# Stores moved to ScalarE's queue, a three-buffer decay pipeline and a gate row summed on GpSimd in a hybrid encoder layer

## The chip, the cores and the metric

The kernel runs on one core of one Trainium2 chip, in one launch. A core has five engines that run their own instruction streams side by side and meet through semaphores: TensorE (PE), VectorE (DVE), ScalarE (ACT), GpSimd (POOL) and SyncE (SP). SP only issues DMA transfers; ACT and POOL can issue them too, each on a queue of its own, in the order of its stream. The metric is the device time of the whole program in microseconds (us), as a median of several runs; less is better.

## What is computed

One layer of a bidirectional hybrid encoder in float32, for 2048 tokens of width 1024. The reference, cut to what the change touches:

```python
mod = c_act @ w_ada[l] + b_ada[l]
shift, scale, gate = jnp.split(mod, 3, axis=-1)
h = rmsnorm(h_res, norm_w[l]) * (1.0 + scale[:, None, :]) + shift[:, None, :]
proj = h @ w_in + b_in
(na_q, na_k, na_v, na_z, ml_q, ml_k, ml_v, ml_o, ml_z, i_f, f_f, i_b, f_b) = jnp.split(proj, split_idx, axis=-1)
na_out = neighbourhood_attention(na_q, na_k, na_v, rpb) * jax.nn.silu(na_z)
qk = jax.nn.silu(centred_short_conv(jnp.concatenate([ml_q, ml_k], axis=-1), conv_w, conv_b))
...
lower = jnp.tril(jnp.ones((L, L), dtype=bool))
Dlog = jnp.where(lower, b[..., :, None] - b[..., None, :] + i_pre[..., None, :], -jnp.inf)
...
S = jnp.einsum('bhntd,bhnsd->bhnts', q, k) * jnp.exp(Dlog - m_t[..., None])
...
hm = (h_fwd + h_bwd).transpose(0, 2, 1, 3) * jax.nn.sigmoid(ml_o).reshape(B, T, ML_HEADS, ML_HEAD_DIM)
...
y = jnp.concatenate([na_out, ml_out], axis=-1) @ w_out
...
h_res = h_res + gate[:, None, :] * y
return rmsnorm(h_res, final_norm_w)
```

`gate` is a row of 1024 numbers, the last third of an adaptive modulation (adaLN); the kernel multiplies it into `w_out` once instead of into every output row. The `exp(Dlog - m_t)` factors, one 64x64 triangle for each chunk, head and direction, are the "decays".

## The kernel before

Every large projection is done in three matmul passes for float32 accuracy: weights and activations are split into a high part (`whi`, `hhi`) and a low part (`wlo`, `hlo`), and hi·hi, lo·hi and hi·lo are added in PSUM (lines 429 to 431). A block of 256 weight columns is loaded in two halves of 512 KB by `load_w` (L193, on SP), ACT makes the high part (L195) and POOL the low part (L196). There are two slots for split weights: `whi_a`/`wlo_a` for even blocks and `whi_b`/`wlo_b` for odd ones, so that the weights of a block are fetched while the block before is computed.

The stages around the change, in PE's order:

- **Start.** Blocks 0 and 1 (mLSTM value and output gate of heads 0 and 1, with the gate columns) run while the rows of x arrive, are normalised (sum of squares on ACT into `junk`, L223) and transposed into `hhi`/`hlo` (L287 to L292). `table_fills` (L538) writes a constant into the bias tables `d_t` in HBM, on SP's queue.
- **Value stage** (`tok_blocks`). Blocks 2 and 3 (`vo_group`: value and output gate of heads 2 and 3) and blocks 4 and 5 (`nav_group`: value of the neighbourhood attention), token-major: 16 tiles of 24 matmuls with 256 columns each. DVE evacuates each tile with a bias (L499, L464) into a staging tile of four (`stvo`, `stv`; two buffers), the output gate gets its sigmoid on ACT (L503), and the staging tile is stored from SP's queue (L506, L468). The store of a group is put off by `defer` and issued by `flush` one group later. After every tile, `next(self.chain)` runs one step of side work: first `gate_chain` (the log-gate arithmetic), then `decays`: for each of 16 groups two broadcast loads (L702, SP), the triangle mask on POOL (L710), eight exponentials (L714) and two stores on ACT's queue (L716), with two buffers. In the steps in between, `gate_row` loads `w_ada`'s gate columns 128 rows at a time into the two halves of `wide` (L401, SP) and sums them on DVE (L408, L410), adds them over partitions with a matmul against a column of ones (L418) and writes the finished row to HBM (`d_gate`); it also copies the final norm weight to `d_fnw`.
- **Convolution** (`conv_blocks`). Blocks 6 and 7 (k) and 8 and 9 (q), channel-major: 8 tiles a block, each 24 matmuls with 512 columns. ACT evacuates a tile with its bias into `u` (L773), DVE passes the two border columns to and from the neighbouring tile (L777, L778) and runs the five taps into `acc` (L806, L808), ACT applies Silu (L809), SP stores the result (L813). For k, PE then transposes it (L819), ACT scales it into `stk` (L821) and SP stores that (L823). A tile's taps need its right neighbour's first columns, so they run a tile later. `conv_step` advances all tiles that are under way by one step. Side work here is `gated_out`: it loads `w_out` in 16 half rows (L737), DVE multiplies the gate in (L744), SP stores the product in `d_wo` (L745). Table rows (`tables_rows`, L551, 72 small copies within HBM, on SP) are spread over blocks 6 to 8.
- **Phase 1b.** The first further projection `pq` (L865) starts right after the last convolution tile. Its weights come by `nq_load` (L830, `rawq`, 512 KB for each 128 columns) and are split by ACT (L838) and POOL (L839) into slot a. The first load is called at the start of block 9, whose own weights are in slot b. The mLSTM scan follows, whose loads `kv` (L1016) and `ck` (L1061) read what the stages before have stored in `d_ck`.

All dependences are found by the tile framework from the tiles' names and buffers; it also orders the instructions of each engine by a model of its own, so that a queue's order in the built program isn't always that of the code. Every DMA of SP and ACT signals one of eight semaphores, taken in turn, and its instruction first waits until the DMA that had that semaphore before has completed.

Of the kernel before, what the change touches and what calls it, by code (L numbers as in the profile page):

```python
# [8 lines left out]
F32 = mybir.dt.float32  # L9
# [6 lines left out]
P = 128  # L16
# [46 lines left out]
class Kernel:  # L63
# [30 lines left out]
    def scratch(self):  # L94
# [10 lines left out]
        self.d_fnw = d.tile([1, D], F32, name="d_fnw")  # L105
        self.d_gate = d.tile([1, D], F32, name="d_gate")
# [284 lines left out]
    def gate_row(self, pool):  # L391

        nc = self.nc
        cact = pool.tile([P, KT], F32, name="cact2")
        nc.sync.dma_start(cact, self.cT)
        nc.scalar.activation(cact, cact, AF.Silu)
        acc = pool.tile([P, D], F32, name="gsum")
        buf = [self.wide[:, :D], self.wide[:, D:]]

        def load(kt):  # L400
            nc.sync.dma_start(buf[kt % 2], self.w_ada[kt * P : (kt + 1) * P, 2 * D : 3 * D])  # L401

        load(0)
        load(1)
        yield
        for kt in range(KT):
            if kt == 0:
                nc.vector.tensor_scalar(acc, buf[0], cact[:, kt : kt + 1], None, ALU.mult)  # L408
            else:
                nc.vector.scalar_tensor_tensor(acc, buf[kt % 2], cact[:, kt : kt + 1], acc, ALU.mult, ALU.add)  # L410
            if kt + 2 < KT:
                load(kt + 2)
            yield
        row = buf[0][0:1]
        nc.sync.dma_start(row, self.b_gate)
        for j in range(2):
            ps = self.sp.tile([P, GT], F32, tag="sp", name=f"gp_{j}")
            nc.tensor.matmul(ps[0:1, :], self.ones[:, 0:1], acc[:, j * GT : (j + 1) * GT], start=True, stop=True)  # L418
            yield
            nc.vector.tensor_add(row[:, j * GT : (j + 1) * GT], row[:, j * GT : (j + 1) * GT], ps[0:1, :])  # L420
        nc.sync.dma_start(self.d_gate, row)
        row = buf[1][0:1]
        nc.sync.dma_start(row, self.fnw)
        nc.sync.dma_start(self.d_fnw, row)

# [31 lines left out]
    def nav_group(self, blk, slot, g):  # L457
# [10 lines left out]
        self.defer(lambda: nc.sync.dma_start(dst, st[:, :, :256]))  # L468
# [16 lines left out]
    def vo_group(self, h, slot, g, first=None):  # L485
        nc = self.nc
        st = self.stage_tile(f"stvo_{h}_{g}")
        nc.gpsimd.memset(st[:, :, 128:129], 1.0)
# [88 lines left out]
    def gate_chain(self, pool, gates):  # L577
# [101 lines left out]
        for i, (name, src) in enumerate((("g", g), ("w", w_r), ("inter", in_r), ("guard", gu_r))):  # L679
            t = self.gtile[:, 1 + i].rearrange("p (d h c) -> p d h c", d=2, h=MH)  # L680
            nc.vector.tensor_copy(t.rearrange("p d h c -> p (d h c)"), transposed(src, f"c_{name}"))
            self.cols[name] = t
            yield

    def decays(self, pool, beside):

        nc = self.nc
        mask = pool.tile([P, 2, CH], F32, name="mask")
# [965 lines left out]
```

## Time and profile before

| | us |
|---|---|
| median of 3 runs | 1388.04 |
| lowest, highest | 1387.38, 1388.36 |
| the profiled execution | 1394.31 |
| its span (first to last instruction) | 1392.3 |
| start: blocks 0, 1 | 0 to 160 |
| value stage: blocks 2 to 5 | 160 to 357 |
| convolution: blocks 6 to 9 | 357 to 554 |
| phase 1b and all that follows | 554 to 1392 |

Times in the profile count from the start of the span. A row of a timeline or of the groups names the line of the code, the engine, the operation, output <- inputs, shapes and the count; in brackets stands how long the engine had been idle before it and what released it. "SPq" and "ACTq" rows are DMA instructions in a queue's issuing engine: their duration is the time the instruction held the queue, not the transfer. The wait table says who waited for whom: total, times, longest.

### The profile page before, as it was taken

Reading aid. Unit: us, or ns where it says so; the run is one execution under the profiler, and the core shown is the slowest. Engines: PE = TensorE matmul, PEld = TensorE weight load, DVE = VectorE, ACT = ScalarE, POOL = GpSimd, SP = SyncE. Lnnn points to the kernel's source line nnn. Section 1 sums busy time; section 2 is a strip of 40 time slices with the busy share of each in tenths; the row PEclk is TensorE's granted clock in tenths of the full one; section 3 lists DMA queues with packets and bytes.
Section 4 is the critical chain, followed back from the end, with each engine's and each line's share of the span. In section 5 each row is a group of like instructions: output and inputs, shape, how many; then the busy total and the mean of one; then the engine's idle time right before and its main releaser. Section 6 shows DMA issues by size and latency. Waiting matters only on the chain.

```text
span 1392.3 us, 23366 instructions
## 1 busy us (share of the span) xinstructions
PE 1307.3 (94%) x8076; PEld 1124.4 (81%) x8076; DVE 823.7 (59%) x2497; ACT 528.7 (38%) x1131; POOL 293.7 (21%) x323
## 2 busy tenths in 40 slices
PE   2989999997999899999999999799998999999996
PEld 2989998987877787888878787688876888888885
DVE  6683323211255559156867777877636776777673
ACT  4642334523233323112323313233335555555551
POOL 4453222424101010001212002112402211111121
PEclk9999999999999999999999999999999999999999
DMA  9799439778458685565766888846687896876872
GB/s 317 224 288 226 121 108 230 187 193 192 135 111 216 145 186 159 170 168 146 201 191 204 247 233 226 211 131 185 177 242 232 188 226 162 198 196 169 190 182 61
DMA packets 269723, 263.68 MB, mean 189 GB/s; under 512 B 33482, under 2 KB 230090, under 8 KB 269606
## 3 DMA queue, kind: packets, MB, share of 16 engines
q1 hardware_dynamic: 178062, 186.45, 50.3%
q0 software_dynamic: 21520, 37.73, 11.0%
q10 hardware_dynamic: 70024, 38.02, 9.7%
q8 instruction: 64, 1.05, 0.3%
q14 instruction: 53, 0.43, 0.1%
HBM read 177.57 MB, written 92.72 MB: 194 GB/s over the span
## 4 chain that ended last, share of the span: by engine, by line
PE 51%; DMA 6%; DVE 4%; issue 3%; ACT 1%; POOL 1%; SPq 0%; ACTq 0%; POOLq 0%; DVEq 0%
PE pq L865 17%; PE y L1435 13%; PE pO L1396 4%; PE pT L1381 4%; DMA kv<-d_ck 3%; PE pc L430 2%; PE pc L431 2%; PE pc L429 2%; PE pS L1353 2%; PE px L1091 2%; PE pi L1093 2%; PE pS L1354 2%; PE dc L1039 1%; DMA d_qna<-qst 1%; PE a L1078 1%
## 5 line engine op out<-in xcount | busy, mean ns | idle before, releaser
L865 PE MATMUL pq<-hhi,whi_a 128*128 128x512 f32 x512 | 208.3, 407 | 2.1 <-ACT whi_a L841 1.3
L865 PE MATMUL pq<-hhi,wlo_a 128*128 128x512 f32 x512 | 208.2, 407 | 0.5 <-DVE wlo_a L842 0.5
L865 PE MATMUL pq<-hlo,whi_a 128*128 128x512 f32 x512 | 208.6, 407 | 0.0
L1360 ACT ACTIVATE pbuf<-pbuf,mn 128x480 f32<-128x480 f32 (+5 forms) x128 | 76.3, 597 | 103.3 <-DVE mn L1359 103.1
L865 PEld LDWEIGHTS pq<-hhi,whi_a 128*128 128x128 f32 x512 | 97.4, 190 | 20.1 <-ACT whi_a L841 1.8
L865 PEld LDWEIGHTS pq<-hhi,wlo_a 128*128 128x128 f32 x512 | 97.3, 190 | 17.8 <-DVE wlo_a L842 1.0
L865 PEld LDWEIGHTS pq<-hlo,whi_a 128*128 128x128 f32 x512 | 97.1, 190 | 16.5
L1435 PE MATMUL y<-hhi,whi_a 128*128 128x512 f32 x256 | 86.1, 405 | 3.1 <-ACT hhi L1334 2.8
L1435 PE MATMUL y<-hhi,wlo_a 128*128 128x512 f32 (+1 forms) x272 | 85.1, 386 | 0.2 <-ACT y L1442 0.2
L1359 DVE CUSTOM_DVE_ANT_0 pbuf<-pS,tab 128x480 f32<-128x480 f32 (+5 forms) x128 | 65.1, 541 | 32.6 <-PE pS L1354 24.2
L839 POOL TENSOR_TENSOR wlo_a<-rawq,whi_a 128x1024 fp32r<-128x1024 f32 x20 | 48.1, 2406 | 165.9 <-ACT whi_a L838 124.2
L1115 POOL TENSOR_TENSOR hm<-hm,ck 128x128 f32<-128x128 f32 x64 | 26.3, 412 | 264.1 <-DVE hm L1114 188.8
L429 PE MATMUL pvo<-whi_b,hhi 128*128 128x256 f32 x256 | 74.8, 292 | 5.3 <-DVE stvo L499 5.3
L1096 ACT ACTIVATE num<-px,gtile 128x129 f32<-128x129 f32 x120 | 38.2, 365 | 99.5 <-PE px L1091 83.5
L1023 DVE TENSOR_SCALAR wv<-kv,gtile 128x129 f32<-128x129 f32 x120 | 39.1, 333 | 60.9 <-DMA kv<-d_ck 31.9
L430 PE MATMUL pvo<-wlo_b,hhi 128*128 128x256 f32 x256 | 73.6, 287 | 0.0
L431 PE MATMUL pvo<-whi_b,hlo 128*128 128x256 f32 x256 | 73.5, 287 | 0.0
L714 ACT ACTIVATE dec<-dec,gtile 128x128 f32<-128x128 f32 x128 | 42.1, 392 | 72.3 <-POOL dec L710 63.4
L499 DVE TENSOR_TENSOR stvo<-pvo,brow 128x256 f32<-128x256 f32 x64 | 26.5, 420 | 70.0 <-PE pvo L431 56.2
L464 DVE TENSOR_TENSOR stv<-pv,brow 128x256 f32<-128x256 f32 x32 | 12.4, 421 | 90.2 <-DMA d_vna<-stv 49.1
L1396 PE MATMUL pO<-pt,v 128*64 128x128 f32 (+3 forms) x832 | 60.8, 282 | 0.0
L1381 PE MATMUL pT<-ident,pbuf 128*128 128x128 f32 (+2 forms) x416 | 59.1, 280 | 0.0
(302 smaller groups left out, 3573.0 us busy)
## 6 DMA issues: line engine op xcount, KB each, us to landing
ck<-d_ck SPq DMA_DIRECT2D x64, 384.5 KB
kv<-d_ck SPq DMA_DIRECT2D x120, 128.5 KB
rawq<-in_w_main_dram SPq DMA_DIRECT2D x28, 512.0 KB
raw<-in_w_main_dram SPq DMA_DIRECT2D x20, 512.0 KB
d_ck<-stvo SPq DMA_DIRECT2D x16, 514.0 KB
x<-in_x_dram SPq DMA_DIRECT2D x16, 512.0 KB
wada<-in_w_ada_dram SPq DMA_DIRECT2D x32, 256.0 KB
dec<-d_mneg SPq DMA_DIRECT2D x32, 256.0 KB
```

Of the source, the lines that this page charges most:

```text
L429: nc.tensor.matmul(ps, lhi(k), rhi(k), start=(k == 0), stop=False)
L430: nc.tensor.matmul(ps, lhi(k), rlo(k), start=False, stop=False)
L431: nc.tensor.matmul(ps, llo(k), rhi(k), start=False, stop=(k == KT - 1))
L714: nc.scalar.activation(t[:, d, o, :], t[:, d, o, :], AF.Exp, bias=self.cols["g"][:, d, h, c : c + 1])
L839: nc.gpsimd.tensor_tensor(lo[:, :, cs], raw, hi[:, :, cs].bitcast(F32), ALU.subtract)
L865: nc.tensor.matmul(patch_ps(ps) if patch else ps, w, self.htok(h, g, k, patch), start=(k == 0 and n == 0), stop=(k == KT - 1 and n == 2))
L1023: nc.vector.tensor_scalar(wv, tiles[d, i][:, 128:257], self.cols["w"][:, d, h, c : c + 1], None, ALU.mult)
L1359: nc.vector.tensor_tensor_reduce(pt[:, :nk], ps, tabs[place[u]][j][:, :nk], 1.0, 3e38, ALU.add, ALU.min, mn)
L1360: nc.scalar.activation(pt[:, :nk], pt[:, :nk], AF.Exp, bias=mn, scale=-1.0, accum_out=sums[:, j : j + 1])
L1381: nc.tensor.transpose(ps[:cs, i, :], pts[j][:, i * cs : (i + 1) * cs], self.ident)
L1396: nc.tensor.matmul(po[j * HD : (j + 1) * HD, :], v[:n, h * HD : (h + 1) * HD], pt[j][:n, i, :], start=(i == 0), stop=(i == nch - 1))
L1435: nc.tensor.matmul(y, m[:, k, :], w[k][:, cs], start=(k == 4 and n == 0), stop=(k == 3 and n == 2))
```

## The change

The gate row leaves the value stage: `gate_row`, `d_gate` and `d_fnw` are gone, and the final norm weight is read from the input when it is used. `gated_out` now begins by loading 16 half rows (128x512) of `w_ada`, and POOL scales and sums them; one matmul against a full matrix of ones for each half sums over partitions and broadcasts, and DVE adds the bias. `w_out`'s halves come after that, so `gated_out` has 32 items instead of 16 and its later ones fall later in the stage.

The decays use a third buffer (the `gsum` tile's tag) and are laid out as a pipeline: a group's load, its mask three steps later and its exponentials and stores five steps later, with a new group every two and a half steps.

The stores `d_vna`, `d_ck<-stvo`, `d_ck<-acc` and `d_ck<-stk` are issued from ACT's queue; those of `stvo` and `acc` right behind the instruction on ACT that makes the tile. The one-column memset of `stvo` goes from POOL to DVE. In the convolution one more step of `gated_out` is taken before each tile, and the k transpose comes one step later.

```diff
--- before.py
+++ after.py
@@ -102,8 +102,6 @@
         self.d_kna = d.tile([2, 512, T], F32, name="d_kna")
         self.d_mix = d.tile([16, P, 4, P], F32, name="d_mix")
         self.d_wo = d.tile([KT, P, D], F32, name="d_wo")
-        self.d_fnw = d.tile([1, D], F32, name="d_fnw")
-        self.d_gate = d.tile([1, D], F32, name="d_gate")
@@ -388,41 +386,6 @@
             pass
         self.flush()
 
-    def gate_row(self, pool):
-
-        nc = self.nc
-        cact = pool.tile([P, KT], F32, name="cact2")
-        nc.sync.dma_start(cact, self.cT)
-        nc.scalar.activation(cact, cact, AF.Silu)
-        acc = pool.tile([P, D], F32, name="gsum")
-        buf = [self.wide[:, :D], self.wide[:, D:]]
-
-        def load(kt):
-            nc.sync.dma_start(buf[kt % 2], self.w_ada[kt * P : (kt + 1) * P, 2 * D : 3 * D])
-
-        load(0)
-        load(1)
-        yield
-        for kt in range(KT):
-            if kt == 0:
-                nc.vector.tensor_scalar(acc, buf[0], cact[:, kt : kt + 1], None, ALU.mult)
-            else:
-                nc.vector.scalar_tensor_tensor(acc, buf[kt % 2], cact[:, kt : kt + 1], acc, ALU.mult, ALU.add)
-            if kt + 2 < KT:
-                load(kt + 2)
-            yield
-        row = buf[0][0:1]
-        nc.sync.dma_start(row, self.b_gate)
-        for j in range(2):
-            ps = self.sp.tile([P, GT], F32, tag="sp", name=f"gp_{j}")
-            nc.tensor.matmul(ps[0:1, :], self.ones[:, 0:1], acc[:, j * GT : (j + 1) * GT], start=True, stop=True)
-            yield
-            nc.vector.tensor_add(row[:, j * GT : (j + 1) * GT], row[:, j * GT : (j + 1) * GT], ps[0:1, :])
-        nc.sync.dma_start(self.d_gate, row)
-        row = buf[1][0:1]
-        nc.sync.dma_start(row, self.fnw)
-        nc.sync.dma_start(self.d_fnw, row)
-
     def mm3(self, ps, lhi, llo, rhi, rlo):
         nc = self.nc
         for k in range(KT):
@@ -465,7 +428,7 @@
             next(self.chain, None)
         self.flush()
         dst = self.d_vna[g * GT : (g + 1) * GT, c0 : c0 + 256].rearrange("(o p) c -> p o c", p=P)
-        self.defer(lambda: nc.sync.dma_start(dst, st[:, :, :256]))
+        self.defer(lambda: nc.scalar.dma_start(dst, st[:, :, :256]))
 
     def load_bias(self, blk):
         self.nc.sync.dma_start(self.brows[blk % 2], self.b_row[0:1, 256 * blk : 256 * blk + 256].broadcast_to([P, 256]))
@@ -485,7 +448,7 @@
     def vo_group(self, h, slot, g, first=None):
         nc = self.nc
         st = self.stage_tile(f"stvo_{h}_{g}")
-        nc.gpsimd.memset(st[:, :, 128:129], 1.0)
+        nc.vector.memset(st[:, :, 128:129], 1.0)
         brow = self.brows[h % 2]
         width = 272 if h == 0 else 256
         for o in range(4):
@@ -502,8 +465,7 @@
             next(self.chain, None)
         nc.scalar.activation(st[:, :, 129:257], st[:, :, 129:257], AF.Sigmoid)
         self.flush()
-        dst = self.d_ck[h, 4 * g : 4 * g + 4, :, 128:385].rearrange("o p c -> p o c")
-        self.defer(lambda: nc.sync.dma_start(dst, st[:, :, 0:257]))
+        nc.scalar.dma_start(self.d_ck[h, 4 * g : 4 * g + 4, :, 128:385].rearrange("o p c -> p o c"), st[:, :, 0:257])
 
 
     def tables_begin(self, pool):
@@ -556,7 +518,7 @@
 
     def tok_blocks(self, chain_pool):
         self.wide = chain_pool.tile([P, 2 * D], F32, name="wide")
-        self.chain = itertools.chain(self.gate_chain(chain_pool, self.gates), self.decays(chain_pool, self.gate_row(chain_pool)))
+        self.chain = itertools.chain(self.gate_chain(chain_pool, self.gates), self.decays(chain_pool))
         order = [2, 3, 4, 5]
         self.tables_begin(chain_pool)
         for n, blk in enumerate(order):
@@ -682,7 +644,7 @@
             self.cols[name] = t
             yield
 
-    def decays(self, pool, beside):
+    def decays(self, pool):
 
         nc = self.nc
         mask = pool.tile([P, 2, CH], F32, name="mask")
@@ -694,7 +656,7 @@
 
         def load(n):
             h, gi = groups[n]
-            flat = pool.tile([P, D], F32, tag=("wgate", "gacc")[n % 2], bufs=1, name=f"dec_{h}_{gi}")
+            flat = pool.tile([P, D], F32, tag=("wgate", "gacc", "gsum")[n % 3], bufs=1, name=f"dec_{h}_{gi}")
             t = flat.rearrange("p (d c t) -> p d c t", d=2, c=4)
             for d in range(2):
                 r = d * 64 + h * NC + 4 * gi
@@ -702,51 +664,69 @@
                 nc.sync.dma_start(flat[:, d * 512 : (d + 1) * 512], src.broadcast_to([P, 512]))
             tiles[n] = t
 
-        load(0)
-        load(1)
-        yield
-        for n, (h, gi) in enumerate(groups):
+        def masked(n):
+            nc.gpsimd.tensor_tensor(tiles[n], tiles[n], mask.unsqueeze(2).broadcast_to([P, 2, 4, CH]), ALU.add)
+
+        def exponent(n):
+            h, gi = groups[n]
             t = tiles.pop(n)
-            nc.gpsimd.tensor_tensor(t, t, mask.unsqueeze(2).broadcast_to([P, 2, 4, CH]), ALU.add)
             for d in range(2):
                 for o in range(4):
                     c = 4 * gi + o
                     nc.scalar.activation(t[:, d, o, :], t[:, d, o, :], AF.Exp, bias=self.cols["g"][:, d, h, c : c + 1])
                 dst = self.d_ck[h, 4 * gi : 4 * gi + 4, :, 641 + d * CH : 641 + (d + 1) * CH].rearrange("c p t -> p c t")
                 nc.scalar.dma_start(dst, t[:, d])
+
+        ends = [5 * n // 2 for n in range(len(groups))]
+        for step in range(ends[-1] + 6):
+            for fn, late in ((exponent, 5), (masked, 3), (load, 0)):
+                if step - late in ends:
+                    fn(ends.index(step - late))
             yield
-            next(beside, None)
-            yield
-            if n + 2 < len(groups):
-                load(n + 2)
-            yield
-        for _ in beside:
-            pass
 
     def gated_out(self, pool):
 
         nc = self.nc
+        cact = pool.tile([P, KT], F32, name="cact2")
+        nc.sync.dma_start(cact, self.cT)
+        nc.scalar.activation(cact, cact, AF.Silu)
         gate = pool.tile([P, D], F32, name="gate")
-        nc.sync.dma_start(gate, self.d_gate.broadcast_to([P, D]))
-        halves = [(k, slice(j * GT, (j + 1) * GT)) for k in range(KT) for j in range(2)]
+        nc.sync.dma_start(gate, self.b_gate.broadcast_to([P, D]))
+        columns = [slice(j * GT, (j + 1) * GT) for j in range(2)]
+        sums = [(kt, j, self.w_ada[kt * P : (kt + 1) * P, 2 * D + j * GT : 2 * D + (j + 1) * GT]) for j in range(2) for kt in range(KT)]
+        halves = [(k, j, self.w_out[:, k, cs]) for k in range(KT) for j, cs in enumerate(columns)]
+        todo = sums + halves
         raws = {}
 
         def load(n):
-            k, cs = halves[n]
-            raws[n] = pool.tile([P, GT], F32, tag="wraw", bufs=2, name=f"wraw_{n}")
-            nc.sync.dma_start(raws[n], self.w_out[:, k, cs])
+            if n < len(todo):
+                raws[n] = pool.tile([P, GT], F32, tag="wraw", bufs=2, name=f"wraw_{n}")
+                nc.sync.dma_start(raws[n], todo[n][2])
 
         load(0)
         load(1)
         yield
-        for n, (k, cs) in enumerate(halves):
+        for n, (k, j, _) in enumerate(todo):
             raw = raws.pop(n)
-            nc.vector.tensor_tensor(raw, raw, gate[:, cs], ALU.mult)
-            nc.sync.dma_start(self.d_wo[k][:, cs], raw)
+            cs = columns[j]
+            if n >= len(sums):
+                nc.vector.tensor_tensor(raw, raw, gate[:, cs], ALU.mult)
+                nc.sync.dma_start(self.d_wo[k][:, cs], raw)
+            elif k == 0:
+                acc = pool.tile([P, GT], F32, tag="gsum", bufs=1, name=f"gsum_{j}")
+                nc.gpsimd.tensor_scalar(acc, raw, cact[:, k : k + 1], None, ALU.mult)
+            else:
+                nc.gpsimd.tensor_scalar(raw, raw, cact[:, k : k + 1], None, ALU.mult)
+                nc.gpsimd.tensor_tensor(acc, acc, raw, ALU.add)
+                if k == KT - 1:
+                    ps = self.sp.tile([P, GT], F32, tag="sp", name=f"gp_{j}")
+                    nc.tensor.matmul(ps, self.ones, acc, start=True, stop=True)
+                    yield
+                    nc.vector.tensor_add(gate[:, cs], gate[:, cs], ps)
             yield
-            if n + 2 < len(halves):
-                load(n + 2)
-            yield
+            load(n + 2)
+            if n >= len(sums):
+                yield
 
 
     def conv_blocks(self, pool):
@@ -767,6 +747,7 @@
                 ct = 2 * pair + sub
                 bias = self.bcol[:, (12 if kind == "q" else 16) + ct : (13 if kind == "q" else 17) + ct]
                 for g in range(NG):
+                    next(self.chain, None)
                     ps = self.pp.tile([P, GT], F32, tag="pp", name=f"pc_{blk}_{sub}_{g}")
                     self.ch_tile(ps, self.wslot[slot], sub, g)
                     last, u = u if g else None, pool.tile([P, GT + 4], F32, tag="u", bufs=4, name=f"u_{blk}_{sub}_{g}")
@@ -807,10 +788,10 @@
             else:
                 nc.vector.scalar_tensor_tensor(acc, src, w, acc, ALU.mult, ALU.add)
         nc.scalar.activation(acc, acc, AF.Silu, bias=self.cb[:, cc : cc + 1])
-        yield
         j = 0 if kind == "q" else 1
         dst = self.d_ck[ct, 4 * g : 4 * g + 4, :, 385 + j * CH : 385 + (j + 1) * CH].rearrange("c p t -> p c t")
-        nc.sync.dma_start(dst, acc.rearrange("p (c t) -> p c t", t=CH))
+        nc.scalar.dma_start(dst, acc.rearrange("p (c t) -> p c t", t=CH))
+        yield
         yield
         if kind == "q":
             return
@@ -820,7 +801,7 @@
         st = self.stage_tile(f"stk_{ct}_{g}")[:, :, 0:128]
         nc.scalar.activation(st, ps.rearrange("p (a q) -> p a q", a=4), AF.Copy, scale=KSCALE)
         d2 = self.d_ck[ct, 4 * g : 4 * g + 4, :, 0:128].rearrange("o p c -> p o c")
-        nc.sync.dma_start(d2, st)
+        nc.scalar.dma_start(d2, st)
 
 
     def nq_load(self, i, s):
@@ -1286,7 +1267,7 @@
 
         def load_fnw():
             fnw.append(self.qst.tile([P, 1032], F32R, tag="st", name="fnw")[:, :D])
-            nc.sync.dma_start(fnw[0].bitcast(F32), self.d_fnw.broadcast_to([P, D]))
+            nc.sync.dma_start(fnw[0].bitcast(F32), self.fnw.broadcast_to([P, D]))
 
         def load_z(b):
             nc.gpsimd.dma_start(zs[pos[b] % 2], self.d_zna[b])
```

## The prediction

> **What bounds the kernel now.** I read the page's engine table first, then a table of stretches cut at the stages (value projections to 357, convolution to 554, then phase 1b), then the waits of 190 to 560, then timelines at the waits found.
>
> ```profile
> PE 1307.3 (94%) x8076; PEld 1124.4 (81%) x8076; DVE 823.7 (59%) x2497; ACT 528.7 (38%) x1131; POOL 293.7 (21%) x323
> ...
> 228.00:250.00 22.00, 17.05 (x127) 16.42 (x125) 8.56 (x9) 9.21 (x23) 4.94 (x4) 0.92 0.78 218
> 250.00:357.00 107.00, 98.17 (x791) 95.56 (x792) 14.95 (x38) 40.77 (x104) 35.70 (x15) 0.97 0.79 193
> 357.00:480.00 123.00, 120.66 (x565) 97.77 (x564) 60.95 (x123) 34.81 (x52) 9.65 (x4) 1.00 0.58 140
> 480.00:500.00 20.00, 17.52 (x73) 13.86 (x72) 13.88 (x22) 7.18 (x10) 5.78 (x2) 0.91 0.70 199
> 500.00:556.00 56.00, 55.22 (x238) 44.50 (x237) 48.17 (x91) 16.55 (x25) 5.00 (x2) 1.00 0.72 176
> ```
>
> TensorE (PE) is the bound, so only its gaps and its reduced clock can be won or lost. The columns are the stretch, its length, the busy time of PE, PEld, DVE, ACT and POOL, PE's granted clock, DMA share, GB/s. Value stage: 22.00−17.05 plus 107.00−98.17 is 13.8 us idle; the clock, 0.08 of 22 and 0.03 of 107, costs 5.0 more: 18.7 (18.8 before rounding) to be won. Convolution: 2.3+2.5+0.8 idle and 0.09×20 of clock: 7.4.
>
> ```profile
> POOL dec L710 <- DMA dec<-d_mneg: 71.1, 11, 13.7
> ...
> ACT dec L714 <- POOL dec L710: 63.4, 13, 13.2
> ...
> DVE stv L464 <- DMA d_vna<-stv: 49.1, 5, 17.0
> ...
> DVE gsum L410 <- DMA wide<-in_w_ada_dram: 23.9, 5, 8.8
> ...
> ACT stk L821 <- DMA d_ck<-stk: 17.6, 7, 5.4
> ...
> PE pv L429 <- DVE stv L464: 8.5, 3, 6.7
> ...
> PE pvo L429 <- DVE stvo L499: 5.3, 3, 2.4
> PE kt L819 <- ACT acc_k L809: 4.8, 5, 2.5
> ...
> PE pq L865 <- ACT u L773: 0.8, 1, 0.8
> ```
>
> (Total, count, longest.) PE's waits 5.3 and 8.5 are the 13.8. The first is DVE's evacuation L499 standing behind a gate-row sum that waits for its weights; the second is L464 waiting for a staging tile whose store is late. Both are seen here:
>
> ```profile
> 230.69 1.28 DVE L410 SCALAR_TENSOR_TENSOR gsum<-wide,cact,gsum 128x1024 f32<-128x1024 f32 x1 [8.82 <-DMA wide<-in_w_ada_dram]
> ...
> 334.34 5.34 SPq L702 DMA_DIRECT2D dec<-d_mneg  x4
> 339.79 0.38 SPq L468 DMA_DIRECT2D d_vna<-stv  x1
> ...
> 346.65 1.42 DVE L464 TENSOR_TENSOR stv<-pv,brow 128x256 f32<-128x256 f32 x4 [16.95 <-DMA d_vna<-stv]
> ```
>
> The store stood on SP's queue behind the decays' loads.
>
> **The change, value stage.** The gate row's 23.9 us of waits leave DVE, and stores go to ScalarE's (ACT's) queue right behind the maker. ACT gains 0.37 us an issue (row at 560.97 below) and has room: 40.77 busy of 107. What is new is that a store stands behind whatever ACT waits for, and DVE, then PE, wait for the store: an exponential waits for POOL's mask for up to 13.2 us now. In the changed program mask and exponential stand three and five column tiles after their load (a tile is 2.8 us: 24 matmuls at half the 0.23 of a wider one), so 8.4 and 14 us, against waits for such loads of 6.5 on the mean (71.1 in 11) and 13.7 at most. Gain: 18.7 at best, 13.8 if the clock isn't won back; a hold of 13.2 on a store, beside the 16.95 that cost PE 6.7, would give back about 3, so 10 if it comes once. I take 16, the middle of the upper two.
>
> A sentence of the Trainium skill (page "Trainium Kernel Development and Optimization", Key Constraints) speaks against this: DMAs of several issuing engines share the same 16 DMA engines, and spreading them saves only issue time. By it the value stage would keep its 18.7 and the sum below would be 16 higher; the row at 339.79 shows instead a wait for a place in one queue.
>
> **Start.** The third table fill moves ahead of the last four x loads on SP, and four square sums of those rows go ahead of `hhi` on ACT.
>
> ```profile
> 92.22 6.33 SPq L538 DMA_DIRECT2D d_t<-big  x2
> ...
> 91.13 0.66 PE L287 MATMUL tp<-ident,x 128*128 128x128 f32 x4 [2.21 <-DVE h L291]
> ```
>
> Fills hold SP 3.2 us each there, and PE already waits in this chain. Bounds 0 (hidden) to 8 (two fills' hold and more of the 2.21); I take +4.
>
> **Convolution within a block.** Stores of `acc` and `stk` (48 of 0.37 us) go to ACT, busy 34.81 of 123, and each k transpose now stands one tile later in PE's order. The `stk` waits of 17.6 and PE's 4.8 shrink. Of 7.4 I take 6 (bounds 3 and 7.4). POOL's gate sums, 30 operations of 128x512, have no row; the nearest are
>
> ```profile
> L839 POOL TENSOR_TENSOR wlo_a<-rawq,whi_a 128x1024 fp32r<-128x1024 f32 x20 | 48.1, 2406 | 165.9 <-ACT whi_a L838 124.2
> L1115 POOL TENSOR_TENSOR hm<-hm,ck 128x128 f32<-128x128 f32 x64 | 26.3, 412 | 264.1 <-DVE hm L1114 188.8
> ```
>
> so between 0.41 and 2.41 us, and 1.2 as half of the larger: 36 us beside some 130 of convolution on a nearly idle POOL, hidden for POOL itself. Without that cover each of the two `gp` matmuls would hold PE for its last sum, 2.4. But a running POOL holds DVE:
>
> ```profile
> 484.20 5.78 POOL L196 TENSOR_TENSOR wlo_b<-raw,whi_b 128x1024 fp32r<-128x1024 f32 x2 [54.31 <-ACT whi_b L195]
> ...
> 484.85 2.86 DVE L808 SCALAR_TENSOR_TENSOR acc_q<-u,cw,acc_q 128x512 f32<-128x512 f32 x1
> 487.63 2.38 DVE L777 COPY u<-u 128x2 f32<-128x2 f32 x1
> ```
>
> One tap and one tiny copy last 2.86 and 2.38 while the two POOL operations run, instead of well under 1. So DVE can lose up to the 36 us in blocks 6 and 7, where it has 123.00−60.95 = 62 to spare. PE feels it only through a k transpose whose taps come late: nothing, or 1.2 for each of 16 tiles, 19. With DVE half idle and the transpose a tile later I take +3, near the lower end. The Trainium skill ("SBUF — State Buffer", section on the two sides) has DVE operations with two SBUF inputs wait out a reading GpSimd operation whole; the tap's row agrees, and by it alone the sum would be nearer the 19.
>
> **The two block boundaries.** This is where I see the price. All DMAs of SP and ACT take one of eight completion semaphores in turn, and a DMA first waits until the one that last had its semaphore has landed, whichever queue issued it. Before, that was nearly always SP's own past. Now every load on SP can stand behind a store that ACT has not reached. That such a wait is real:
>
> ```profile
> 236.41 1.57 ACT L714 ACTIVATE dec<-dec,gtile 128x128 f32<-128x128 f32 x5 [5.98 <-DMA raw<-in_w_main_dram]
> ```
>
> ACT's decay store, and the exponentials behind it, waited 5.98 us for SP's weight load. And that late loads reach PE:
>
> ```profile
> 469.80 6.12 DMA d_wo<-wraw
> ...
> 476.38 0.38 SPq L193
> 476.86 8.00 DMA raw<-in_w_main_dram
> ...
> 485.90 0.67 ACT u L773
> ...
> 488.13 0.43 PE pc L430
> ...
> 491.12 0.42 PE pc L431
> 491.54 0.23 PE pc L429
> ```
>
> A 256 KB store takes 6.12 here, a weight load 8.00, load and split 9.0 (476.86 to 485.90), and after the stall nine matmuls (488.13 to 491.54) run at 0.43 instead of 0.23, 1.8 us.
>
> Block 8 to 9: in the changed program SP's load of block 9's weights waits for ACT's store of `acc_q_1_1` (sixth of block 8's eight tiles) and stands behind table rows that wait for its predecessors. That store needs the seventh tile's evacuation, which starts one tile, 24×0.23=5.6, before block 8's last matmul ends (t1), then taps, Silu and issue. Evacuation 0.7, five taps of 0.72, a Silu taken as long as the evacuation, and issue 0.4 are 5.4; the last tile of the convolution took 8.7 for this (553.5 to 562.19, below). So it is issued at t1−0.2 to t1+3.1 and lands 3 (half of 6.12) to 6 later; load and split 7.5 (511.35 to 518.80, below) to 9.0, POOL's difference 2.4: PE resumes at t1+13 to 20. I take 14, since the 8.7 holds work of the next phase; with the clock +16, bounds 13 to 21. ACT's split also stands behind the rest of block 8's ACT work, over by about t1+6, so that decides nothing.
>
> Convolution to phase 1b: the first `rawq` load, issued 42 us ahead now,
>
> ```profile
> 511.35 0.63 SPq L830 DMA_DIRECT2D rawq<-in_w_main_dram  x1
> ...
> 518.80 2.52 POOL L839 TENSOR_TENSOR wlo_a<-rawq,whi_a 128x1024 fp32r<-128x1024 f32 x1 [28.82 <-ACT whi_a L838]
> ...
> 553.58 0.69 ACT L773 ACTIVATE u<-pc,bcol 128x512 f32<-128x512 f32 x1 [2.20 <-PE pc L431]
> ...
> 562.19 0.36 SPq L813 DMA_DIRECT2D d_ck<-acc_q  x1
> ...
> 420.40 17.12 SPq L551 DMA_DIRECT2D d_t<-d_e  x22
> ...
> 560.97 0.37 ACTq L899 DMA_DIRECT2D d_zml<-qst  x1
> ```
>
> stands after the change behind eight table rows, the first of which waits for the very last conv store, `acc_q_3_3`, to land, and behind one `w_out` load. From the last conv matmul's end (t0, 553.5 before): last store issued at t0+5.4 to 8.7; landing 3 to 6; eight rows at 17.12/22=0.78, 6.2; one more issue, 0.8; load and split 7.5 to 9.0; difference 2.4: 25 to 33. I take 29 and allow 24 to 36. PE waited 0.8 here before, so +28 and 1.8 of clock: +30 (24 to 38). Later `rawq` and `kv` loads move back as much, but so do their users.
>
> **Sum.** −16−6+4+3+16+30 = +31. The profiled execution took 1394.31 (span 1392.3), so 1425; the median of the runs, 1388.04, lies 6.3 under it: 1419. Own range: −18.7−7.4+0+0+13+24 = +11 at the least, 1399; all terms at their worst give −10−3+8+19+21+38 = +73, which they won't reach together, so I stop at +57, 1445.
>
> **Rivals.**
> (A) Faster: the semaphores don't hold SP, because ACT's stores are long landed when SP gets there, and both loads arrive in time. For it: loads run 42 us ahead now, and PE paces everything. Against it: the order names the last conv store itself ahead of `rawq`. Decides: a `rawq` issue before the last conv matmul. −16−6+4+3 = −15: 1373.
> (B) Only one boundary stalls: with the end alone −15+30 = +15, 1403; with block 9 alone +1, 1389. For it: at block 9 one earlier store would be enough to free the load.
> (C) The stores behind ACT bring the value stage nothing: exponentials hold ACT as they did (63.4), staging tiles come free as late. +31+16 = +47, 1435. For it: DMA share is 0.79 there, loads may stay slow. Against: two tiles' more lead. The page's rule named under the value stage would come out here.
> (D) The gate sums hold DVE at every k transpose: 19 in place of 3, +47, 1435 too. For it: two POOL operations to each sum and up to two sums a tile. Against: DVE's 62 us to spare.
>
> **How the numbers follow.** Forecast 0.62, A 0.12, B 0.12 (half of it near no change), C 0.08, D 0.06. Differences under 0.2%, 2.8 us, cannot be told from none. Faster: A and a little of B, 0.14; same 0.04; slower 0.82. The range 1386 to 1445 holds B's lower case, the own range and C and D; A is left out.
>
> **What would show it.** Right: PE waits of some 14 and 28 us, ahead of the first matmul of block 9 and of the first `pq`, put down to the new weights' split on ACT or POOL; SP's `rawq` issue after ACT's last `acc_q` store; no wait of `stv` for `d_vna` near 17; no `gsum` on DVE; clock 1.00 up to the boundary. Wrong: `rawq` issued during block 9 (A), an idle ACT ahead of exponentials and PE gaps in 230 to 357 (C), `kt` or `gp` waits of PE on DVE or POOL in blocks 6 to 8 (D).

## The result and the profile after

| | before | after |
|---|---|---|
| median of 6 runs, us | 1388.20 | 1424.59 |
| lowest to highest | 1387.36 to 1393.72 | 1414.54 to 1430.95 |
| span of the profiled execution | 1392.3 | 1412.7 |

The change makes the kernel slower: ratio 1.0249, 95% interval 1.0203 to 1.0295, which is 28 to 41 us. The profiled execution of after, 1414.54, is the fastest of its six runs, and that of before, 1394.31, lay above its own median; so the two traces differ by only 20.4 us of span, against 36.4 between the medians. The rows below explain the traces; the rest of the 36.4 isn't explained, nor is what makes the runs of after spread over 16 us.

The table of stretches of after, cut as the prediction cut it and with one stretch more (columns: stretch, length, busy PE, PEld, DVE, ACT, POOL, granted clock, DMA share, GB/s):

```profile
228.00:250.00 22.00, 22.00 (x187) 22.00 (x187) 3.21 (x10) 13.22 (x27) 8.58 (x4) 1.00 0.89 198
250.00:357.00 107.00, 102.68 (x825) 101.31 (x824) 13.66 (x35) 37.91 (x95) 36.81 (x16) 0.97 0.80 185
357.00:480.00 123.00, 119.27 (x534) 95.92 (x533) 79.58 (x137) 36.19 (x56) 48.88 (x30) 0.97 0.48 135
...
500.00:556.00 56.00, 47.10 (x191) 36.91 (x191) 34.10 (x64) 12.85 (x18) 6.66 (x4) 0.91 0.48 140
556.00:650.00 94.00, 69.72 (x319) 56.51 (x318) 28.97 (x77) 13.37 (x18) 9.57 (x4) 0.87 0.64 192
```

The value stage is better: PE's idle time there falls from 13.8 to 4.3, and with the clock (0.03 of 107, 3.2) the loss from 18.7 to 7.5. The loss has moved right: 8.9 idle in 500 to 556, where before had 0.8, and 24.3 after 556. PE's waits in after say on whom:

```profile
PE pq L846 <- ACT whi_a L819: 22.9, 1, 22.9
...
PE pc L392 <- ACT whi_b L193: 5.8, 1, 5.8
PE gp L723 <- POOL gsum L720: 5.5, 2, 3.7
...
PE tp L285 <- DVE x L228: 4.9, 1, 4.9
PE pv L392 <- DVE stv L427: 4.3, 1, 4.3
```

The two boundary stalls of the forecast are the two largest new waits. The chain of waits of after shows the second as the prediction set it out, step by step:

```profile
558.51 2.66 DVE acc_q L789 x4
...
563.52 3.34 DMA d_ck<-acc_q
566.87 0.61 SPq L513
...
572.10 0.46 SPq L704
...
573.12 5.82 DMA rawq<-in_w_main_dram
...
579.03 1.07 ACT whi_a L819
...
580.16 2.37 POOL wlo_a L820
```

The last convolution store (L793, on ACT) has to land before SP's first of eight table rows goes; the `w_out` load and store (L704, L714) follow, and `rawq` only then. In the trace this store and the first of these rows signal the same semaphore, and so do the store and the load at block 9's boundary, shown below. The first `pq` starts at 580.14, 25.8 later than the 554.32 of before. The matmuls behind it are slow at first, so that the 25th starts 29.3 later (589.3 against 560.0); some 9 of these come back by the end, in part by fewer waits in the scan (`dc` 5.0 and `a` 1.7, where before has 6.3 and 4.3). That this coupling acts all along the convolution, and not only at its end, stands in SP's own timeline. Before, 22 table rows held SP 17.12 us; in after

```profile
413.51 75.02 SPq L513 DMA_DIRECT2D d_t<-d_e  x16
```

16 of them take 75.02, and SP's part of the wait table names what they waited for, stores of ACT's queue:

```profile
SPq L513 <- DMA d_ck<-stk: 32.0, 5, 10.3
...
SPq L513 <- DMA d_ck<-acc_q: 24.3, 6, 7.2
```

Block 9's boundary, from the chain of waits and from ACT's timeline:

```profile
498.80 3.20 DMA d_ck<-acc_q
502.06 3.90 DMA raw<-in_w_main_dram
```

```profile
506.63 0.72 ACT L790 ACTIVATE acc_q<-acc_q,cb 128x512 f32<-128x512 f32 x1 [1.51 <-DVE acc_q L789]
...
507.85 2.00 ACT L193 ACTIVATE whi_b<-raw 128x1024 fp32r<-128x1024 f32 x2 [0.50 <-ACT acc_q L790]
```

The load waits for ACT's store as forecast, but lands at 505.96. The split could have begun there; it begins at 507.85, behind block 8's last Silu. So ACT's order, not the load, has the last word by 1.9 us.

The start lost 4.6 (the `tp` wait of 4.9, where before has 0.3), not by the table fill. DVE's timeline and ACT's:

```profile
67.11 0.16 DVE L1186 TENSOR_SCALAR nwt_x<-nwt_x 128x4 f32<-128x4 f32 x1 [6.19 <-issue]
67.14 0.06 DVE L451 MEMSET stvo<- 128x4 f32 x1
```

```profile
56.89 0.40 ACTq L468 DMA_DIRECT2D d_ck<-stvo  x1
```

The memset of the ones column, which the change moved from POOL to DVE, waits for its staging tile to be free, that is for the store issued at 56.89. While it waits, 6.19 us, DVE's normalisation of x stands behind it, and PE's transposes behind that.

### The profile page after: what moved, and what is told of

It is laid out like the page before. It is cut to its first block, busy times and chain, and to the rows that moved or that the text cites. A ratio compares the mean times of both kernels' runs of the same rounds, so it can differ in the third digit from the quotient of the medians.

```text
span 1412.7 us, 23340 instructions
## 1 busy us (share of the span) xinstructions
PE 1308.8 (93%) x8076; PEld 1127.0 (80%) x8076; DVE 814.4 (58%) x2505; ACT 527.5 (37%) x1129; POOL 337.0 (24%) x337
## 3 DMA queue, kind: packets, MB, share of 16 engines
q0 software_dynamic: 21520, 37.73, 10.9%
## 4 chain that ended last, share of the span: by engine, by line
PE 72%; DMA 11%; POOL 5%; DVE 4%; issue 4%; ACT 2%; SPq 1%; ACTq 0%; POOLq 0%; DVEq 0%
PE pq L846 21%; PE y L1416 12%; PE pO L1377 4%; PE pT L1362 4%; PE pc L394 3%; PE pc L393 3%; PE pc L392 3%; PE pvo L394 2%; PE pvo L392 2%; PE pvo L393 2%; DMA d_ck<-dec 2%; PE pvo L445 2%; PE pi L1074 2%; PE px L1072 2%; DMA dec<-d_mneg 2%
## 5 line engine op out<-in xcount | busy, mean ns | idle before, releaser
L846 PE MATMUL pq<-hhi,whi_a 128*128 128x512 f32 x512 | 209.2, 409 | 22.9 <-ACT whi_a L819 22.9
L668 POOL TENSOR_TENSOR dec<-dec,mask 128x1024 f32<-128x1024 f32 x16 | 38.2, 2391 | 109.4 <-DMA dec<-d_mneg 89.5
```

What stands on the lines that cost most here:

```text
L668: nc.gpsimd.tensor_tensor(tiles[n], tiles[n], mask.unsqueeze(2).broadcast_to([P, 2, 4, CH]), ALU.add)
L846: nc.tensor.matmul(patch_ps(ps) if patch else ps, w, self.htok(h, g, k, patch), start=(k == 0 and n == 0), stop=(k == KT - 1 and n == 2))
```

## The experiments

Ratios are against runs of before on the same chip in the same job (its median was 1379.69 in the job of f1, f4 and f7, 1390.86 in that of f6), so ratios are compared, not times.

### The boundaries: is it the stores on ACT's queue?

**e5**: before, with only the convolution's stores moved (and the k transpose a step later, as in the change).

```diff
-        yield
         dst = self.d_ck[ct, 4 * g : 4 * g + 4, :, 385 + j * CH : 385 + (j + 1) * CH].rearrange("c p t -> p c t")
-        nc.sync.dma_start(dst, acc.rearrange("p (c t) -> p c t", t=CH))
+        nc.scalar.dma_start(dst, acc.rearrange("p (c t) -> p c t", t=CH))
+        yield
...
-        nc.sync.dma_start(d2, st)
+        nc.scalar.dma_start(d2, st)
```

> The kernel before with only the convolution's stores on ACT's queue behind their maker (and the k transpose a step later); gate row, decays and value stores as before, no sums on POOL. Theory: the k waits of 7 go, block 9 waits 10 to 22 and the first pq 20 to 28, so slower than before by 25 to 40: 1413 to 1428. Rival (POOL's gate sums cost it): no loss, 1381 to 1389.

Measured: 1428.11 (1424.62 to 1431.85), ratio 1.0286 (1.0265 to 1.0307). These few lines alone cost as much as the whole change, at the upper edge of the theory's range. From its waits and SP's timeline:

```profile
PE pq L865 <- ACT whi_a L838: 21.9, 1, 21.9
...
PE pc L429 <- ACT whi_b L195: 18.3, 1, 18.3
```

```profile
444.76 64.14 SPq L551 DMA_DIRECT2D d_t<-d_e  x16
```

SP is held by the table rows again, with no gate sum and no `w_ada` load in the convolution.

**e10**: before with these stores on GpSimd's queue (`nc.gpsimd.dma_start` for both; the k transpose stays where it was). In the trace GpSimd's DMAs signal eight semaphores of their own.

> The kernel before with the convolution's stores issued on POOL's queue in place of SP's. As in the run with these stores on ACT, they leave SP's order, and the weight loads of block 9 and of the first pq stand on SP behind the same table rows; but POOL's transfers signal on semaphores of their own, so SP's instructions no longer wait for them. Theory (the waits across queues make the stalls): block 9 and the first pq wait under 2 us, the k waits of 7 shrink, 1379 to 1389. Rival (the loads are late because they come behind the table rows in SP's order): block 9 waits over 10 and pq over 15 as with the stores on ACT, 1413 to 1430.

Measured: 1407.61 (1403.26 to 1411.39), ratio 1.0124 (1.0079 to 1.0168), between the two expectations. The loads are early, so the waits across queues made them late, and not their place behind the table rows; the stalls shrink but stay, and both are equal:

```profile
PE pq L865 <- ACT whi_a L838: 7.4, 1, 7.4
PE pc L429 <- ACT whi_b L195: 7.4, 1, 7.4
```

```profile
441.46 3.32 SPq L193 DMA_DIRECT2D raw<-in_w_main_dram  x2
...
528.47 0.63 SPq L830 DMA_DIRECT2D rawq<-in_w_main_dram  x1
```

```profile
504.75 0.72 ACT L809 ACTIVATE acc_q<-acc_q,cb 128x512 f32<-128x512 f32 x1 [1.51 <-DVE acc_q L808]
505.38 1.99 ACT L195 ACTIVATE whi_b<-raw 128x1024 fp32r<-128x1024 f32 x2
```

Block 9's weights are issued 64 us ahead of their split and the split still runs right behind the stage's last Silu: in the built order it stands there. If ACT has this order in e5 too, e5's stalls are 7.4 of it plus what the late load adds, an estimated 18.3−7.4 = 10.9 and 21.9−7.4 = 14.5. Moving the stores to another queue changes the order of ACT's splits as well as the time of the loads. For block 9 the forecast named this order and put it at nothing; for the first `pq` it didn't have it.

**e1**: the changed kernel with the convolution's stores back on SP (`nc.sync` in both lines).

> The changed kernel with the convolution's stores (acc, stk) back on SP's queue; everything else of the change stays. Theory (SP's weight loads stand behind ACT's convolution stores at two places): both boundary stalls go, the first pq waits under 2 us and block 9 under 2 us; the value stage keeps its gain of about 11, the start its loss of 2, the two gp matmuls theirs of 8, so about 1388, the same as before within 5. Rival (the gate sums on POOL, which hold DVE, are what costs): nothing in that is changed, so still over 1410.

Measured: 1406.98 (1404.45 to 1407.27), ratio 1.0121 (1.0106 to 1.0136), outside both expectations. Taking the convolution's stores back from ACT undoes half of the loss; it does not bring the kernel to before. Its weights are in time, and new waits have come:

```profile
PE pq L846 <- ACT u L754: 7.8, 1, 7.8
...
PE kt L800 <- ACT acc_k L790: 6.3, 3, 3.0
...
PE pc L392 <- ACT u L754: 3.8, 2, 2.8
```

```profile
499.22 15.66 SPq L513 DMA_DIRECT2D d_t<-d_e  x24
```

SP issues 24 table rows in one go, and the `w_out` loads and the stores wait behind them; DVE's gate multiply (L713) waits for its load, and the taps, Silu and `u` stand behind it. The gate row takes 16 of `gated_out`'s now 32 items, so the `w_out` halves fall into the q blocks and compete there.

**e2** and **e3**: the changed kernel with only the first `rawq` load, or only block 9's loads, on GpSimd's queue.

```diff
+        (nc.sync if i else nc.gpsimd).dma_start(raw, self.w_main[10 + s // 2, :, :, (s % 2) * P : (s % 2 + 1) * P])
...
+            (nc.gpsimd if blk == 9 else nc.sync).dma_start(raw, self.w_main[blk, :, 4 * half : 4 * half + 4, :])
```

> The changed kernel with only the first rawq load issued on POOL's queue. Theory: the 22.9 us wait ahead of the first pq goes and with it 1.2 on the difference and 1.6 of clock; the second rawq load still stands on SP behind the last convolution store and makes PE wait 2 to 6 at the second pq tile; about 1403 (1398 to 1409), while block 9 still waits 5 to 10. Rival (ACT's split itself is late because ACT is full of stores): the first pq still waits over 15, about 1424.

> The changed kernel with only block 9's two weight loads issued on POOL's queue. Theory: the waits of 5.8 and 1.3 at block 9 go with 3 of clock, the wait ahead of the first pq stays at 20 to 27: 1414 (1410 to 1419). Rival (ACT's split is late by ACT's own order): block 9 still waits about 6, 1424.

Measured: e2 1421.67, ratio 1.0233 (1.0189 to 1.0278); e3 1419.84, ratio 1.0215 (1.0184 to 1.0246), both longer than the theory had it. Each removes its own stall, and little is won, because SP's queue is late as a whole. In e2 the first `pq` waits 0.8, and the second `rawq` load takes its place (a `pq` wait of 13.4, more than expected). In e3 block 9 starts in time, and the first `pq` waits 31.9 instead of 22.9.

### The value stage: what brought the gain?

**e6**: before, with only the value stage's stores on ACT and the memset on DVE.

> The kernel before with only the value stage's stores on ACT's queue (and the small memset on DVE); gate row and decays as before. Theory (the late stores on SP cost 8.5 of waits of pv and 2 of clock; the gate row another 5.3 and 2): the pv waits shrink by half or more, the pvo waits of 5 stay: 1380 to 1386. Rival (the stores only change what holds them, ACT's exponentials in place of SP's loads): no gain, 1386 to 1392.

Measured: 1406.77 (1401.76 to 1409.81), ratio 1.0102 (1.0064 to 1.0141), slower. Its `pv` waits are 11.3 and its `pvo` waits 7.3, against 8.5 and 5.3 before. Its wait table and DVE's timeline show both reasons:

```profile
ACT dec L713 <- POOL dec L709: 59.4, 11, 12.4
```

```profile
239.39 0.06 DVE L488 MEMSET stvo<- 128x4 f32 x1 [6.89 <-DMA d_ck<-stvo]
```

The exponentials go on waiting for the mask, 59.4 here in the value stage against 63.4 before, and the stores now stand behind them; and the memset on DVE waits for such a store, with the evacuations behind it. At the start the memset shows too, in a `tp` wait of 6.3. The stores on ACT and the memset together lose, which is more than the rival C of the prediction took from the stores; how much each of the two loses isn't shown, since no run moves the stores of before alone.

**e7**: e6 with the three decay buffers and the new steps; the gate row stays in the value stage on DVE (in half rows, summed in `wide`).

> The kernel before with the value stage of the change (stores on ACT, decays in three buffers as a pipeline) and its own convolution. The gate row stays in the value stage on DVE, in half rows with twice the lead, since its sum no longer has room in the decays' third buffer; the final norm weight is read directly. Theory (the value stage gains 11, the boundaries lose only by the convolution's stores): no boundary stalls, 1374 to 1383. Rival (the gate row's place is what gains in the value stage): 1384 to 1390.

Measured: 1390.93 (1389.08 to 1397.59, 10 runs), ratio 1.0017 (0.9996 to 1.0039): the same as before, and not the gain of the theory. `pv` waits 7.4, `pvo` 5.7. The pipeline, with the gate row in half rows, makes up for what e6 loses. The value stage of after differs from this one only by the gate row's place, so its gain comes when the gate row leaves. The memset is on DVE here too, with a `tp` wait of 5.9; e7 with the memset on POOL was not run, so it is open whether these parts could beat before.

**e11**: e7 with the convolution's stores on GpSimd's queue, as in e10.

> The two together: that value stage, and the convolution's stores on POOL's queue. Theory: the gains add, 1368 to 1380, the fastest of all. Rival (POOL's store issues collide with DVE's taps or with the splits of weights on POOL): slower than the value stage alone.

Measured: 1411.74 (1408.67 to 1415.43), ratio 1.0151 (1.0114 to 1.0189), slower than e7, and the two boundary waits are 7.4 and 7.4 again. ACT's order costs this much with either value stage.

### All stalls out of the way

**f1**: the changed kernel with the memset back on POOL.

> The changed kernel with only the memset of stvo back on POOL. Theory (on DVE it waits in order for the staging tile's store and holds the square roots of x behind it): the wait of 4.9 near 65 us goes to under 1, about 5 us less, 1416 to 1424 beside 1424.6. Rival (the table fill ahead of the x loads causes it): the wait stays 4 to 6.

Measured: 1415.38, ratio 1.0238 (1.0197 to 1.0279). The `tp` wait falls from 4.9 to 0.2, so the memset is its cause, and `pv` waits fall from 4.3 to 2.8. The total is not told apart from the changed kernel's 1.0249.

**f4**: f1 with block 9's loads and the first four `rawq` loads on GpSimd's queue and four steps more ahead of each `gp` matmul.

> The changed kernel with all that its stalls stand behind taken away, its stores staying on ACT: block 9's weights and the first four rawq loads on POOL's queue, the memset of stvo back on POOL, four more steps between a gate sum and its matmul. Theory (loads behind waits across queues, and the splits that ACT's order then puts after the block, cost 36; gp waits 8; the memset in DVE's order 5): block 9, first pq and gp wait under 2 each, 1370 to 1385, faster than before. Rival (the stall only moves, now to the scan's loads, which SP still issues behind the last stores): 1388 to 1405.

Measured: 1416.20 (1412.90 to 1421.79), ratio 1.0258 (1.0218 to 1.0297). Between 190 and the convolution's end PE waits 2.9 in all, and the first `pq` runs at 529.98, 50 us before that of after. The time is the same, and outside both expectations. The chain of waits in phase 1b:

```profile
660.83 2.77 DMA wraw<-in_w_out_dram
...
664.44 2.00 DMA d_wo<-wraw
...
666.59 0.32 SPq L999
...
666.96 2.14 DMA kv<-d_ck
...
669.12 0.80 PE dc L1022 x2
```

`w_out`'s last halves are still going through their two buffers, load, multiply, store, load, and SP's first `kv` load (L999) stands behind them. They are late by the same wait across queues, in a new place. SP's timeline:

```profile
530.47 76.57 SPq L513 DMA_DIRECT2D d_t<-d_e  x19
```

These 19 table rows hold SP to 607, and SP's wait table puts 59.8 us of it, in nine waits, down to `d_zml`, the stores that ACT issues in phase 1b in every version. In this version the rows come up among these stores, and 12 of the 16 `w_out` loads are still to be issued when the convolution ends. The scan's first `dc` runs at 669.1; in after at 625.5, before at 596.1. What PE gained by an early `pq` it lost by a late scan: `dc` waits of 17.4 and `a` waits of 9.6 (6.3 and 4.3 before), and a granted clock of 0.93 from 650 to 850, where before has 1.00.

**f7**: f4 with the value stage's stores back on SP.

> The same with the value stage's stores back on SP's queue, put off by a group as before. Theory (it is the gate row's leaving that freed the value stage, not the queue of the stores): the value stage loses as little, within 3 us of the run with the stores on ACT. Rival (the stores' queue is what gained): pv waits of 8 or more come back, 5 to 10 us longer.

Measured: 1439.04 (1432.15 to 1441.52), ratio 1.0411 (1.0370 to 1.0452). Here the stores on ACT are worth 1.5%, more than either expectation had (the `pv` wait is 9.3 against 1.9 in f4, the first `pq` waits 10.8 and the gate sums end after 550). Between f4 and f7 they help; in e6, with the gate row in the stage, the old decays and the memset on DVE, they come with a loss. The value of a queue depends on what stands in it; which of these three differences decides isn't shown.

**f6**: e1 with the memset on POOL, four steps more ahead of `gp`, and the table rows issued by GpSimd.

> The changed kernel with the convolution's stores back on SP as in e1, the memset on GpSimd as in f1, four more steps ahead of each gp matmul, and the table rows (L513) issued by GpSimd. Theory (e1's remaining loss is SP's own queue: 24 table rows issued in one go hold the wraw loads and, through DVE's multiply, taps, Silu and the k transposes): the kt wait on acc_k (6.3 in e1) and the pc wait on u (3.8) fall under 1 each, gp and the wait near 65 us under 1, so ratio near 1.00 (0.995 to 1.006); a rest of up to 8 at the first pq may stay, since the split of the second rawq tile stands behind the last Silu in ScalarE's order. Rival (the rows are not what holds it: it is the number of steps that gate row and w_out now take, and DVE's multiply waits for wraw in any case): kt and pc waits stay as in e1, 5 to 10 in sum, ratio 1.008 to 1.012.

Measured: 1412.63 (1407.78 to 1415.86), ratio 1.0155 (1.0104 to 1.0205). The `kt` and `pc` waits are gone and `gp` waits 0.4, as the theory on SP's rows had it; the total misses both expectations. The convolution's last taps now stand behind the `w_out` chain:

```profile
545.08 2.71 DMA wraw<-in_w_out_dram
547.81 0.69 DVE wraw L713
...
549.11 2.66 DVE acc_q L791 x4
```

The first `pq` waits 7.5 for the last `u`, the first `dc` behind it 10.7 for its load, and 540 to 560 holds only 2.19 us of PE work. No version tried beats before; e7 equals it.

## Why the prediction was right, and where not

The mechanism, the sign and the size of the whole came out: 1419 was said, with 1386 to 1445, and 1424.59 measured. That the size fits so well is in part luck. The terms below miss by up to 6 us, both ways, and cancel; and the sum of +31 was made for the traces, whose spans differ by 20.4, while the medians differ by 36.4. Of the signs that it named, the `rawq` issue behind ACT's last store and the absence of `gsum` on DVE came; the two waits were 5.8 and 22.9 in place of 14 and 28, a `stv` wait of 14.8 stayed, and the clock was 0.97 from 250 to 480. By its steps:

- **Conv to phase 1b, +30**: right in its path, a little high in its sizes. The last store goes 6.3 after the last matmul's end (5.4 to 8.7 was said), lands in 3.34 (3 to 6), eight rows take 5.2 (6.2), load and split 7.0 (7.5 to 9.0). POOL's low part takes 2.4, but PE starts ahead of it and waits 1.2 for it later. So `pq` starts 22.9 after the last convolution matmul, where 25 to 33 was said. With the slower matmuls behind it PE loses 25.7 more than before, inside 24 to 38.
- **Block 8 to 9, +16**: 10.4, below its bounds of 13 to 21 (and with the `gp` wait of 1.8 that stands inside this stall, still below). The step that failed is that ACT's split behind block 8's ACT work "decides nothing". The load came 3.90 after it was issued, not 7.5 to 9.0 with the split, and then ACT's order did decide. e10 shows this order by itself: 7.4 with the weights there long before.
- **Value stage, −16**: −11.2. The `pvo` waits for the gate row are gone, as forecast, and the size is near the lower one it gave: the hold that the prediction priced as "10 if it comes once" did come once, a staging store behind exponentials and a `stv` wait of 14.8. The memset on DVE, which was not costed, took some of the rest (in f1 `pv` waits fall by 1.5). That stores behind their maker bring anything by themselves isn't shown: e6 loses with them and the memset, and f4 against f7 gains with the gate row away, the new decays and the memset on POOL.
- **Convolution within a block, −6**: right. The `kt` waits of 4.8, the `stk` waits of 17.6 and the slow matmuls behind them are gone, 6.6 of the 7.4 counted. The later transpose wasn't needed for it: e10 and e11 don't have it and show no `kt` wait, while e1, with it and the stores on SP, has 6.3.
- **Gate sums on POOL, +3**: 8.5, mis-sized, and at another place. The priced slowdown of DVE shows but is hidden. Groups of DVE in 357 to 480, before and then after:

```profile
L808 DVE SCALAR_TENSOR_TENSOR acc_k<-u,cw,acc_k 128x512 f32<-128x512 f32 x61 | 44.9, 781 | 0.3
L806 DVE TENSOR_SCALAR acc_k<-u,cw 128x512 f32<-128x512 f32 x16 | 7.7, 482 | 4.5 <-DMA d_ck<-acc_k 4.4
```

```profile
L789 DVE SCALAR_TENSOR_TENSOR acc_k<-u,cw,acc_k 128x512 f32<-128x512 f32 x64 | 54.3, 894 | 0.6
L787 DVE TENSOR_SCALAR acc_k<-u,cw 128x512 f32<-128x512 f32 x16 | 11.4, 709 | 0.0
```

  Taps got 113 ns and first taps 227 ns longer on the mean, 64×0.113+16×0.227 = 10.9 us in all, and no k transpose waited. That POOL is the cause is argued, not tested; for it, the q block's taps in the same window, run while POOL stood idle, took 744 and 482 on the mean. The price came at the two `gp` matmuls, which hold PE until the last sum is there: 5.5 of waits and 3 of slower clock behind them. The prediction named this ("each of the two `gp` matmuls would hold PE for its last sum, 2.4") and took it as covered. For the first (3.7) the cover was too short, since POOL worked almost without a break from 360 to 385.6. For the second (1.8) its loads came late on SP; that wait lies inside block 9's stall and so cost little by itself. The groups of POOL in 357 to 510

```profile
L719 POOL TENSOR_SCALAR wraw<-wraw,cact 128x512 f32<-128x512 f32 x14 | 25.1, 1795 | 80.3 <-DMA wraw<-in_w_ada_dram 80.3
L720 POOL TENSOR_TENSOR gsum<-gsum,wraw 128x512 f32<-128x512 f32 x14 | 18.9, 1349 | 1.1
```

  show 80.3 us of waiting for `w_ada`, 79.0 of it ahead of the very last row, and 1.8 and 1.35 us an operation where 1.2 was taken.
- **Start, +4**: 4.6, and the agreement is luck: the cause was the memset and not the table fill (f1).
- **Not seen**: that the `w_out` chain runs past the convolution's end, with the scan's first `kv` load behind it. Of its 16 loads, 8 are still to be issued there in after and none in before. The doubled list of `gated_out` doesn't explain it: e1 has that list and none left, e5 has the old list and 7 left. The hold of SP by the table rows does; in e10, whose rows don't wait for stores, 6 are left, as SP waits up to 56.1 for a gate multiplication on DVE. In after all this is hidden behind the larger stalls; f4 uncovers it. What the doubled list does by itself shows in f6, where the last taps wait for it.

Of the rivals, A is excluded (`rawq` went after the last convolution matmul) and B too (both boundaries stall). C did not come out, as the value stage gained 11.2, though e6 shows what its condition, exponentials that hold ACT, can cost. D came in its sign, but at `gp`; no `kt` waited. The sentence of the Trainium skill ("Trainium Kernel Development and Optimization", Key Constraints) that another issuing engine saves only issue time is not borne out here in either direction: 48 stores moved cost 2.9% in e5, and the value stage's stores are worth 1.5% between f7 and f4.

## What to carry to other kernels

When a store moves to another engine's queue, read the built order of the loads that stay behind: here every SP instruction could wait for an ACT store, and 16 small copies, which took 0.78 us each before, held SP for 75 us. At a stage boundary look also at the place of the weight split in its engine's order; in e10 an early load was of no use to a split that stood behind the last activation of the stage. When one stall is taken out, read the same queue again: in f4 the table rows came to wait for phase 1b's stores in place of the convolution's, and SP was held for 76.57 us, with all that stood behind.

## What had not been expected of the hardware

A memset of 0.06 us on 4 columns held DVE, and through it PE, because it had to wait for a DMA store; with it on POOL, at the same place in the program, PE's wait was 0.2 in place of 4.9. And an earlier start of PE's next stage by 50 us (529.98 against 580.14) gave no time at all, because the loads of the stage behind it were on the queue that stayed late.
